# A decoder layer on one core: side loads on GpSimd's queue, and the cache rows copied from memory to memory

## The chip, the cores and the metric

The kernel runs on one core of one Trainium2 chip. Its time is the device time of one execution in microseconds (us). The core has a matrix engine (PE), a vector engine (DVE), a scalar engine (ACT), GpSimd (POOL) and a sync engine (SP) that here only issues DMAs. Each engine takes its instructions in a fixed order and waits at each for the semaphores that it needs. All DMAs of the core are carried by the same 16 DMA engines. Those that SP issues appear in the profile as queue q1 (`hardware_dynamic`), those that GpSimd issues as queue q0 (`software_dynamic`).

## The reference

One layer of a hybrid decoder, for a prompt of 256 tokens and a group of 8 sample tokens which share the weights, all in float32. Cut to what matters here:

```python
h = _rmsnorm(x, norm_mix)
q, k, v, z, xbc, dt, qm, g = jnp.split(h @ w_in, ...)         # one input projection
a_out = _swa_attend(q, k_all, v_all, ...)                     # window 128, grouped queries
s_out, conv_new, h_new = _ssd(xbc, z, dt, state_conv, state_ssm, ...)
m_out = _mem_attend(qm, mem_k, mem_v)                         # 256 memory tokens
merged = g0 * (a_out @ w_up_swa) + g1 * (s_out @ w_up_ssd) + g2 * (m_out @ w_up_mem)
x = x + merged @ w_out
y = x + (silu(h2 @ w_gate) * (h2 @ w_up)) @ w_down            # h2 = rmsnorm(x)
# of the sample group:
k_all = concat([cache_swa_k, k], axis=1); s_swa_k = k_all[:, 1:]   # 127 old rows move up by one
v_all = concat([cache_swa_v, v], axis=1); s_swa_v = v_all[:, 1:]
s_ssm = decay * state_ssm + dt * x * B                              # 32 x 64 x 128 per token
```

Each of the eight sample tokens has its own sliding-window cache (128 rows of 256 numbers for keys and as many for values), memory cache (256 rows of 1024 for keys and for values) and recurrent state. The outputs `s_swa_k` and `s_swa_v` are the window caches moved up by one row, with the new row at the end.

## The kernel before

**The stream.** The work on the weights is a list of units. A unit is a `raw` tile of 128 x 1024 numbers (512 KB), issued on SP in line L230. ACT copies it to `hi` (L167) and DVE computes `lo` (L168), which split each number in two parts of reduced precision. Then PE runs 24 products of 128 x 128 by 264 columns (L146; for the memory keys and values 12 of 512 columns). `feed` issues loads four units ahead and splits up to three ahead; there are four `raw`, three `hi` and three `lo` buffers. The order of the stream is: memory keys and values (`pmem`), the input projection (`pin`) with the branches' projections (`pua`, `pum`, `pus`) among it, then `pout` (w_out), and the feed-forward groups (`pg`, `pu`, `pdn`).

**The side work.** Norms, attention and the recurrent scan run beside the stream. They are generators in two queues, `side` and `slow`; after each unit they advance by a little. Their loads are the side loads: `x` for the norm (L408, 4 DMAs of 512 KB), and those of the generator `ahead` (L556), which fetches two tiles ahead: 32 tiles of the memory caches into `lm` buffers, and 4 tiles of the window caches and 16 of the recurrent state into `ld` buffers. In the notes below the state tiles are called j0 to j15. All of these are issued on SP, among the loads of weights. GpSimd issues the stores and the small loads and re-loads: `out_dram<-ld` (L1229) stores an updated state tile, `bb` and `cbs` (L1216, L1217) and `dec` (L1155) are broadcast reads, `mg_d`, `mgi`, `sg_d` and `sig` carry the gates and the merged sum out to DRAM and back, `xg` and `xgs` (L1438, L1440) fetch x again for the w_out stage.

**The rows that move up.** In `swa` (the window attention), the sample's key cache comes in two `ld` tiles of four tokens each, with the 128 rows on partitions; the value cache does the same later. As soon as such a tile is there, `move_rows` (L520) stores its partitions 1 to 127 to rows 0 to 126 of the output, on GpSimd.

**What sets the order.** The program is written in the order of the generators, but the instructions of every engine are then placed by a scheduler that plays the program through on its own costs. An engine's list is therefore fixed when the program is built, and it is not the order of the text: a load or a store is put where that planning had it ready. The two buffers `ld` hold in turn window-cache tiles and state tiles; a state load waits for the store of the tile two before it, since it reuses that buffer. A DMA of GpSimd also waits for the eighth DMA before it on that queue, with which it shares a semaphore.

Of the kernel before, what the change touches and what calls it, by code (L numbers as in the profile page):

```python
# [20 lines left out]
NP = 256          # prompt tokens  # L21
NS = 8            # sample tokens
NT = NP + NS      # columns of every activation
# [4 lines left out]
# column offsets of w_in  # L28
# [7 lines left out]
class Side:  # L36
    """Work that runs beside the stream of weights: tasks in a fixed order, a little after each unit."""
# [25 lines left out]
    def drain(self, name):  # L63
        """Everything up to and with the task of that name."""
        while any(t[0] == name for t in self.tasks):
            g = self._head()
            assert g is not None, (name, self.tasks[0])
            sum(g)
            self.tasks.pop(0)
# [3 lines left out]
def tile_hybrid_decoder_step(  # L73
# [42 lines left out]
    class Feat:  # L116
        """16 tiles of features, hi and lo, each [P, NT]"""
# [34 lines left out]
    def rsqrt(v, n, parts=P, alloc=None):  # L152
        """v ** -0.5 of positive v: an estimate from the exponent, then three Newton steps."""
        alloc = alloc or tiny
        y = alloc("rs_y", n)[0:parts]
        a = alloc("rs_a", n)[0:parts]
        V.tensor_scalar(y.bitcast(I32), v.bitcast(I32), 1, None, op0=ALU.logical_shift_right)
        V.tensor_scalar(y.bitcast(I32), y.bitcast(I32), -1.0, MAGIC, op0=ALU.mult, op1=ALU.add)
        for _ in range(3):
            V.tensor_tensor(a, y, y, op=ALU.mult)  # L160
            V.scalar_tensor_tensor(a, a, -0.5, v, op0=ALU.mult, op1=ALU.mult)
            V.scalar_tensor_tensor(y, a, 1.5, y, op0=ALU.add, op1=ALU.mult)
        return y

    def split(hi, lo, src):
        """src = hi + lo exactly, each with the 12 bits of float32r."""
        act(hi, src, AF.Copy)  # L167
        V.tensor_tensor(lo, src, hi.bitcast(F32), op=ALU.subtract)  # L168

    # ------------------------------------------------------------ constants  # L170
# [6 lines left out]
    # ------------------------------------------------------------ loads of the start  # L177
# [40 lines left out]
    # ------------------------------------------------------------ the stream of weights  # L218
# [40 lines left out]
    def group(name, loads, nk, xh, xl, after, perm=False, before=None):  # L259
        """Four output tiles: the sum over nk tiles of features of w^T x."""  # L260
        st = {}

        def prod(u):
            def f(hi, lo):
                if u == 0:
                    if before:
                        before()
                    st["ps"] = [dps(name)[:, 0:NT] for _ in range(4)]
                for c in range(4):
                    for k in range(2):  # L270
                        kk = 2 * u + k
                        wh = hi[:, k * 512 + c * P:k * 512 + (c + 1) * P]
                        wl = lo[:, k * 512 + c * P:k * 512 + (c + 1) * P]
                        mm(st["ps"][c], wh, xh(kk), start=kk == 0, stop=False)
                        mm(st["ps"][c], wh, xl(kk), start=False, stop=False)
                        mm(st["ps"][c], wl, xh(kk), start=False, stop=kk == nk - 1)
            return f

        for u in range(nk // 2):
            units.append(dict(  # L280
                loads=loads(u), perm=perm, prod=prod(u),
                after=(lambda: after(st["ps"])) if u == nk // 2 - 1 else None))
# [4 lines left out]
    # ------------------------------------------------------------ memory keys and values  # L287
# [112 lines left out]
    # ------------------------------------------------------------ h = RMSNorm(x), features on partitions  # L400
    hh, hl = Feat("hh"), Feat("hl")

    def prep_x():
        x_t = {}
        for h in range(2):
            for t in range(2):
                m = (lm if t else ld)("x")
                nc.sync.dma_start(m, x_prompt[0, t * P:(t + 1) * P, h * 1024:(h + 1) * 1024])  # L408
                x_t[t, h] = m
                yield 1.3  # L410
# [33 lines left out]
    # ------------------------------------------------------------ the other constants  # L444
    tri = const([P, P], "tri")              # tri[s, l] = l >= s
    nd = const([P, 256], "nd")              # -(distance) of a block's queries to the last 256 keys
# [16 lines left out]
    def consts():  # L463
# [36 lines left out]
        # the sample's convolution over its state  # L500
# [17 lines left out]
    def move_rows(dst, b, tile_):  # L518
        """Rows of a cache that move up by one, of four tokens of the sample."""
        nc.gpsimd.dma_start(dst[0, b:b + 4, 0:127].rearrange("b t h d -> t b (h d)"), tile_[1:128])  # L520


    # ------------------------------------------------------------ input projection
# [25 lines left out]
    # ---- the caches and the state, loaded ahead in the order in which they are used  # L549
    def ahead(sources, pool, depth):  # L550
        tiles = []
        for n in range(len(sources)):
            while len(tiles) < min(n + depth, len(sources)):
                b, src = sources[len(tiles)]
                t = pool("ld")
                nc.sync.dma_start(t.rearrange("p (b c) -> p b c", b=b) if b else t, src)  # L556
                tiles.append(t)
            yield tiles[n]
# [8 lines left out]
    # ---- memory attention  # L567
    def mem_prompt_work():
        qm = qt["qm"]
        # mean squares of the queries  # L570
# [16 lines left out]
        # the sample's, a row per token and head  # L587
# [20 lines left out]
        # the sample's queries as rows, and to all partitions  # L608
# [9 lines left out]
        # prompt  # L618
# [40 lines left out]
    def mem_sample_work():  # L659
        rq, qd = mT["rq"], mT["qd"]  # L660
        # scores by the vector engine, a key per partition
# [29 lines left out]
    def mem_sample_values():  # L691
        pT = mT["p"]
        po = sps("oms")
        for b in range(NS):
            # the heads' outputs of token b in row b of the heads' strips of 32 partitions
            w = t1("pb")[:, 0:256].rearrange("p (mc h e) -> p mc h e", mc=2, h=4)
            V.memset(w.rearrange("p mc h e -> p (mc h e)"), 0.0)
            V.tensor_copy(w[:, :, :, b], pT.rearrange("p (mc b h) -> p mc b h", mc=2, b=NS)[:, :, b])
            for mc in range(2):
                vc = next(mem_loads)  # L700
                for h in range(4):
                    mm(po[32 * h:32 * h + 32, 0:256], w[:, mc, h], vc[:, h * 256:(h + 1) * 256],
                       start=b == 0 and mc == 0, stop=b == NS - 1 and mc == 1)
                yield 1.5
# [11 lines left out]
    # ---- sliding-window attention  # L716
# [19 lines left out]
    def swa_keys():  # L736
        kvt = kvT["t"]
        # keys and values with tokens on partitions
# [47 lines left out]
    def swa():  # L786
# [3 lines left out]
        # mean squares of the queries  # L790
# [31 lines left out]
        # prompt  # L822
# [55 lines left out]
        # sample  # L878
        pT_s = sps("sTs")
        kcs = {}  # L880
        for b in range(NS):
            if b % 4 == 0:
                kc = next(other_loads).rearrange("p (b c) -> p b c", b=4)
                move_rows(s_swa_k, b, kc)
# [19 lines left out]
        # -(distance) of the sample to the cache  # L904
# [27 lines left out]
        for b in range(NS):  # L932
            if b % 4 == 0:
                vc = next(other_loads).rearrange("p (b c) -> p b c", b=4)
                move_rows(s_swa_v, b, vc)
            # a strip of 32 partitions for each token, its 16 heads first
            mm(po[32 * (b % 4):32 * (b % 4) + 32, b // 4], pT[:, 16 * b:16 * b + 32], vc[:, b % 4])
# [19 lines left out]
    # ------------------------------------------------------------ SSD  # L957
    ssd = {}
    dt_tok = const([P, 64], "dt_tok")
    last = const([P, 11, 24], "last")       # the raw rows that the next step's convolution needs  # L960
# [5 lines left out]
    def conv(ct, raw, dst):  # L966
        """dst = silu(conv(raw) + b) of the four tiles of channels from ct on; the last raw rows go out."""
# [61 lines left out]
    def softplus(x, n, rows):  # L1029
        """log(1 + exp(x)) = max(x, 0) + 2 atanh(u / (2 + u)), u = exp(-|x|)."""  # L1030
# [16 lines left out]
    def task_dt():  # L1047
# [16 lines left out]
        # sample: heads on partitions, then each head's values on the partitions of its channels  # L1064
# [19 lines left out]
        # cumulative sums of dt * a within the chunks  # L1084
# [9 lines left out]
        # weights of the states  # L1094
# [10 lines left out]
    def ssd_chunk_work(g):  # L1105
# [20 lines left out]
        # states  # L1126
# [55 lines left out]
    def ssd_norm_work(g):  # L1182
# [8 lines left out]
        # 64 tokens in each strip of 32 partitions  # L1191
# [106 lines left out]
    # ------------------------------------------------------------ gates and the branches' projections  # L1298
# [78 lines left out]
    # order of the stream  # L1377
# [55 lines left out]
    # ------------------------------------------------------------ x + merged @ w_out  # L1433
# [44 lines left out]

    for i in range(4):
        group("pout", w_loads(w_out[0], 512 * i), KT, lambda k: mg[k // 4][:, k % 4], lambda k: mg[k // 4][:, 4 + k % 4], after_out(i),  # L1480
              before=lambda i=i: load_x(i))

    # ------------------------------------------------------------ SwiGLU
# [61 lines left out]
    # ------------------------------------------------------------ run the stream  # L1545
# [65 lines left out]
```

## Time and profile before

| what | us |
|---|---|
| median of 3 runs | 2030.79 (2026.6 to 2030.96) |
| profiled execution, span from first to last instruction | 2028.6 |
| PE busy | 1947.4 (96%) |
| DVE busy | 1159.9 (57%) |
| ACT busy | 970.5 (48%) |
| POOL busy | 103.0 (5%) |
| moved by SP's DMAs (q1) | 353.5 MB |
| moved by GpSimd's DMAs (q0) | 45.0 MB |

The profile page gives the profiled execution's span and no other time of its own; the span lies 2.2 us under the median of the runs. A busy PE is an upper figure, since the ends of its pipelined products are modelled. What PE loses shows in three ways: as idle time, as a granted clock below 1, and as fewer instructions in a stretch of time. In the views by stretch a row has the stretch, its length, busy time (and number of instructions) of PE, PE's weight loads, DVE, ACT and POOL, the granted clock, the busy share of the DMA engines, and GB/s.

### The profile page before, as it was taken

The numbers are of one execution on the slowest core, as the hardware profiler recorded it, in microseconds if no ns is written. First come the engines' busy times: TensorE is split into PE (matmuls) and PEld (weight loads), VectorE is DVE, ScalarE is ACT, GpSimd is POOL, SyncE is SP. The second block draws the span as 40 slices with busy tenths as digits, with TensorE's granted clock in tenths as the row PEclk, the third lists the DMA queues.
The fourth block names the chain that finished last, engine by engine and source line by source line (L and its number), as shares of the span: only waits on it lengthen the run. The fifth ranks groups of instructions, "written<-read, shape, count | busy, mean of one in ns | idle before, by whom it ended". The sixth has DMA issues, their size and how long they took to land.

```text
span 2028.6 us, 37670 instructions
## 1 busy us (share of the span) xinstructions
PE 1947.4 (96%) x15436; PEld 1880.1 (93%) x15436; DVE 1159.9 (57%) x2217; ACT 970.5 (48%) x1419; POOL 103.0 (5%) x187
## 2 busy tenths in 40 slices
PE   8989999996999879899999999999999999999999
PEld 6778898885999779899999999999999999999998
DVE  5634667653667657568745556555544555445553
ACT  6634445753666556564544454444333444334443
POOL 2011000010001000111000000000000000000000
PEclk9999999997999889899999999999999999999999
DMA  8656666666758786978755555666556665556653
GB/s 276 197 184 172 227 210 222 189 183 214 207 158 240 208 225 199 244 238 292 246 177 191 194 175 169 179 185 177 183 181 178 181 179 180 185 179 179 184 186 130
DMA packets 214750, 400.90 MB, mean 198 GB/s; under 512 B 21143, under 2 KB 41798, under 8 KB 214440
## 3 DMA queue, kind: packets, MB, share of 16 engines
q1 hardware_dynamic: 193792, 353.50, 56.8%
q0 software_dynamic: 20784, 44.99, 8.2%
q8 instruction: 121, 1.98, 0.4%
q14 instruction: 53, 0.43, 0.1%
HBM read 374.45 MB, written 24.06 MB: 196 GB/s over the span
## 4 chain that ended last, share of the span: by engine, by line
PE 82%; DMA 10%; DVE 3%; issue 2%; ACT 2%; POOL 0%; SPq 0%; ACTq 0%; POOLq 0%; DVEq 0%
PE pin L146 22%; PE pu L146 13%; PE pdn L146 13%; PE pg L146 13%; PE pout L146 5%; PE pus L146 5%; PE pmem L146 5%; DMA ld<-in_state_ssm_dram 4%; PE pum L146 2%; DMA raw<-in_w_in_dram 2%; DVE lo L168 1%; DMA ld<-in_cache_mem_v_dram 1%; DVE ld L1225 1%; ACT hi L167 1%; PE po L146 1%
## 5 line engine op out<-in xcount | busy, mean ns | idle before, releaser
L168 DVE TENSOR_TENSOR lo<-raw,hi 128x1024 fp32r<-128x1024 f32 (+1 forms) x626 | 747.3, 1197 | 689.6 <-ACT hi L167 686.4
L167 ACT ACTIVATE hi<-raw 128x1024 fp32r<-128x1024 f32 (+1 forms) x626 | 645.4, 1036 | 883.2 <-PE pin L146 189.9
L146 PE MATMUL pin<-hh,hi 128*128 128x264 f32 x1728 | 499.9, 292 | 40.1 <-ACT hi L167 37.7
L146 PE MATMUL pin<-hl,hi 128*128 128x264 f32 x1728 | 497.6, 290 | 0.0
L146 PE MATMUL pin<-hh,lo 128*128 128x264 f32 x1728 | 487.7, 290 | 6.1 <-DVE lo L168 5.8
L146 PEld LDWEIGHTS pin<-hh,hi 128*128 128x128 f32 x1728 | 332.7, 193 | 47.4 <-ACT hi L167 39.9
L146 PEld LDWEIGHTS pin<-hh,lo 128*128 128x128 f32 x1728 | 325.7, 192 | 10.7 <-DVE lo L168 8.7
L146 PEld LDWEIGHTS pin<-hl,hi 128*128 128x128 f32 x1728 | 332.4, 192 | 3.3 <-issue 2.5
L146 PE MATMUL pdn<-fah,hi 128*128 128x264 f32 x704 | 200.0, 285 | 0.0
L146 PE MATMUL pdn<-fal,hi 128*128 128x264 f32 x704 | 199.7, 285 | 0.0
L146 PE MATMUL pu<-h2h,hi 128*128 128x264 f32 x704 | 199.7, 285 | 0.0
L146 PE MATMUL pu<-h2l,hi 128*128 128x264 f32 x704 | 199.5, 285 | 0.0
L146 PE MATMUL pg<-h2l,hi 128*128 128x264 f32 x704 | 199.3, 285 | 0.0
L146 PE MATMUL pg<-h2h,hi 128*128 128x264 f32 x704 | 198.7, 284 | 0.0
L146 PE MATMUL pdn<-fah,lo 128*128 128x264 f32 x704 | 197.3, 285 | 0.0
L146 PE MATMUL pu<-h2h,lo 128*128 128x264 f32 x704 | 196.9, 285 | 0.0
L146 PE MATMUL pg<-h2h,lo 128*128 128x264 f32 x704 | 196.4, 285 | 0.0
L146 PEld LDWEIGHTS pdn<-fah,hi 128*128 128x128 f32 x704 | 132.9, 189 | 0.1
L146 PEld LDWEIGHTS pu<-h2h,hi 128*128 128x128 f32 x704 | 132.9, 189 | 0.0
L146 PEld LDWEIGHTS pu<-h2l,hi 128*128 128x128 f32 x704 | 132.8, 189 | 0.0
L146 PEld LDWEIGHTS pdn<-fal,hi 128*128 128x128 f32 x704 | 132.7, 189 | 0.1
L146 PEld LDWEIGHTS pg<-h2h,hi 128*128 128x128 f32 x704 | 132.8, 189 | 0.0
(504 smaller groups left out, 2954.4 us busy)
## 6 DMA issues: line engine op xcount, KB each, us to landing
raw<-in_w_in_dram SPq DMA_DIRECT2D x218, 512.0 KB, 4.9
raw<-in_w_gate_dram SPq DMA_DIRECT2D x88, 512.0 KB, 3.7
raw<-in_w_up_dram SPq DMA_DIRECT2D x88, 512.0 KB, 4.1
raw<-in_w_down_dram SPq DMA_DIRECT2D x88, 512.0 KB, 3.8
raw<-in_w_mem_kv_dram SPq DMA_DIRECT2D x32, 512.0 KB, 5.1
raw<-in_w_up_ssd_dram SPq DMA_DIRECT2D x32, 512.0 KB, 3.8
raw<-in_w_out_dram SPq DMA_DIRECT2D x32, 512.0 KB, 3.7
ld<-in_cache_mem_k_dram SPq DMA_DIRECT2D x16, 512.0 KB, 5.0
```

Source lines behind the costliest of these rows:

```text
L146: nc.tensor.matmul(out, lhsT=lhsT, rhs=rhs, start=start, stop=stop)
L167: act(hi, src, AF.Copy)
L168: V.tensor_tensor(lo, src, hi.bitcast(F32), op=ALU.subtract)
L1225: V.scalar_tensor_tensor(h[:, b], bb[:, b], dx[:, b:b + 1], h[:, b], op0=ALU.mult, op1=ALU.add)
```

## The change

All side loads go out on GpSimd's queue, so that SP issues weights alone (and, as before, the first loads of the memory prompt and the last stores). `move_rows` no longer stores from the tiles; it copies both caches from DRAM to DRAM, once each, and is called from the w_out groups. The diff, without the comments that were dropped and with the lines around cut:

```diff
     def prep_x():
...
-                nc.sync.dma_start(m, x_prompt[0, t * P:(t + 1) * P, h * 1024:(h + 1) * 1024])
+                nc.gpsimd.dma_start(m, x_prompt[0, t * P:(t + 1) * P, h * 1024:(h + 1) * 1024])
...
-    def move_rows(dst, b, tile_):
-        nc.gpsimd.dma_start(dst[0, b:b + 4, 0:127].rearrange("b t h d -> t b (h d)"), tile_[1:128])
+    def move_rows():
+        for dst, src in ((s_swa_k, cache_swa_k), (s_swa_v, cache_swa_v)):
+            to, of = (t[0].rearrange("b t h d -> b (t h d)")[:, o:o + 127 * 256].rearrange("b (s e) -> s b e", s=16)
+                      for t, o in ((dst, 0), (src, 256)))
+            tc.keep_in_program_order(nc.gpsimd.dma_start(to, of))
...
     def ahead(sources, pool, depth):
...
-                nc.sync.dma_start(t.rearrange("p (b c) -> p b c", b=b) if b else t, src)
+                nc.gpsimd.dma_start(t.rearrange("p (b c) -> p b c", b=b) if b else t, src)
...
     def swa():
...
                 kc = next(other_loads).rearrange("p (b c) -> p b c", b=4)
-                move_rows(s_swa_k, b, kc)
...
                 vc = next(other_loads).rearrange("p (b c) -> p b c", b=4)
-                move_rows(s_swa_v, b, vc)
...
+    def before_out(i):
+        load_x(i)
+        if i == 3:
+            move_rows()
+
     for i in range(4):
         group("pout", ..., after_out(i),
-              before=lambda i=i: load_x(i))
+              before=lambda i=i: before_out(i))
```

Since the scheduler places every instruction anew, the lists of the engines tell where things now stand. SP has 632 rows where it had 688. In these lists a row has the line, the operation and out<-in with the numbers of the buffers, and what stands behind them is the shape.

The first place is GpSimd's list where the window attention's key tiles are stored. Before, the two stores of 127 partitions (L520) stood between the stores of the memory values `vm` and ahead of the sample's queries `qd`:

```order
L371 DMA out_dram<-km_687 128x512
L350 DMA out_dram<-vm_109 128x512 x2
L520 DMA out_dram<-ld_4425 127x4x256
L350 DMA out_dram<-vm_109 128x512 x2
L520 DMA out_dram<-ld_4427 127x4x256
L615 DMA qd<-qrow_1850 32x128 x2
```

And now:

```order
L371 DMA out_dram<-km_687 128x512
L559 DMA ld_4425<-in_cache_swa_k_dram 128x4x256
L559 DMA ld_2340<-in_cache_mem_k_dram 128x1024
L350 DMA out_dram<-vm_109 128x512 x4
L559 DMA ld_4427<-in_cache_swa_k_dram 128x4x256
L559 DMA ld_2342<-in_cache_mem_k_dram 128x1024
L618 DMA qd<-qrow_1850 32x128 x2
```

The stores of 127 partitions are gone, and the loads of the tiles stand in their place. The same holds for the value tiles further on.

The second place is the third group of up_mem, where GpSimd re-loads the merged sum (`mgi`), 23 rows before the end of its list. The two copies from DRAM to DRAM (L523) now stand here, ahead of the re-load for up_mem's third group:

```order
L1349 DMA mgi_9898<-mg_d 128x1056
L1441 DMA xgs_13187<-in_x_sample_dram 8x512
L1441 DMA xgs_13480<-in_x_sample_dram 8x512
L523 DMA out_dram<-in_cache_swa_k_dram 16x8x2032
L523 DMA out_dram<-in_cache_swa_v_dram 16x8x2032
L1349 DMA mgi_10150<-mg_d 128x1056
L1355 DMA mg_d<-sig_9897 128x1056
L1349 DMA mgi_10316<-mg_d 128x1056
```

Although the text calls them in the w_out stage, they wait for nothing that is computed, and the scheduler put them this early; before, `mgi` followed the two `xgs` directly.

The third place is the recurrent state of group 1 (tiles j6 to j9). On SP, the loads of the state stood among those of the weights; that piece before:

```order
L230 DMA raw_7750<-in_w_in_dram 128x2x512
L556 DMA ld_7519<-in_state_ssm_dram 128x8x128
L230 DMA raw_7780<-in_w_in_dram 128x2x512
L556 DMA ld_7703<-in_state_ssm_dram 128x8x128
L230 DMA raw_7841<-in_w_in_dram 128x2x512
L230 DMA raw_7879<-in_w_in_dram 128x2x512
L556 DMA ld_8387<-in_state_ssm_dram 128x8x128
L230 DMA raw_7910<-in_w_in_dram 128x2x512
```

Now they stand on GpSimd, among the stores of the tiles and the broadcast reads (j7 is `ld_7515`, j8 `ld_7699`, j9 `ld_8383`; the numbers moved by four):

```order
L1372 DMA mg_d<-sig_7365 128x1056
L559 DMA ld_7515<-in_state_ssm_dram 128x8x128
L1230 DMA out_dram<-ld_7282 128x8x128
L1230 DMA out_dram<-ld_7515 128x8x128
L1217 DMA bb_8379<-bc_d 128x8x128
L559 DMA ld_7699<-in_state_ssm_dram 128x8x128
L1218 DMA cbs_8380<-bc_d 128x8x128
L559 DMA ld_8383<-in_state_ssm_dram 128x8x128
L1156 DMA dec_8067<-acs_d 128x8x128
```

The load of j7 now stands ahead of the store of j6, that of j8 behind the store of j7. On ACT the first operation on j8 and on j9 moved back behind some splits of weights; before:

```order
L1224 ACTIVATE ld_7519<-ld_7519,dsc 128x128 x8
L167 ACTIVATE hi_7752<-raw_7720 128x1024
L998 ACTIVATE raw_7810<-pin_7542 128x264
L998 ACTIVATE raw_7810<-pin_7543 128x264
L1224 ACTIVATE ld_7703<-ld_7703,dsc 128x128 x3
L998 ACTIVATE raw_7810<-pin_7544 128x264
L1224 ACTIVATE ld_7703<-ld_7703,dsc 128x128 x5
```

and now, with j8 behind the copies of the projection's result (`raw_7806`, the raw input of the convolution):

```order
L1225 ACTIVATE ld_7515<-ld_7515,dsc 128x128 x8
L167 ACTIVATE hi_7670<-raw_7638 128x1024
L167 ACTIVATE hi_7718<-raw_7668 128x1024
L167 ACTIVATE hi_7748<-raw_7716 128x1024
L999 ACTIVATE raw_7806<-pin_7538 128x264
L972 ACTIVATE acc_7812<-raw_7806,vbc,cw 128x264
L999 ACTIVATE raw_7806<-pin_7539 128x264
L999 ACTIVATE raw_7806<-pin_7540 128x264
L167 ACTIVATE hi_7778<-raw_7746 128x1024
L999 ACTIVATE raw_7806<-pin_7541 128x264
L972 ACTIVATE acc_7812<-raw_7806,vbc,cw 128x264 x3
L167 ACTIVATE hi_7839<-raw_7776 128x1024
```

j7's operation moved forward by two splits, and those on j8 and j9 follow the last row here.

## The prediction

> **What bounds the kernel now.** I began with the page's span and the shares of the chain that ended last, then cut the span into stretches, and read the DMA view, the chain in order of time and the waits of each stretch that loses.
>
> ```profile
> span 2028.6 us, 37670 instructions
> PE 82%; DMA 10%; DVE 3%; issue 2%; ACT 2%; POOL 0%; SPq 0%; ACTq 0%; POOLq 0%; DVEq 0%
> ```
>
> PE's products are the bound; a tenth of the chain is transfers that PE could not wait out. The view by stretch (columns: stretch, length, busy time and instructions of five engines, granted clock, DMA share, GB/s) says where:
>
> ```profile
> core 0: us, PE busy (x) PEld busy (x) DVE busy (x) ACT busy (x) POOL busy (x), PEclk, DMA share, GB/s
> 112.00:193.00 81.00, 71.49 (x539) 66.69 (x538) 29.81 (x50) 28.03 (x41) 10.29 (x4) 0.94 0.58 170
> 429.00:476.00 47.00, 29.01 (x248) 25.37 (x247) 18.19 (x45) 15.96 (x23) 9.41 (x3) 0.82 0.60 148
> 640.00:682.00 42.00, 32.38 (x263) 31.02 (x262) 21.39 (x51) 20.86 (x44) 4.88 (x6) 0.91 0.80 197
> 720.00:752.00 32.00, 19.69 (x154) 18.88 (x153) 14.50 (x44) 15.69 (x38) 3.52 (x4) 0.90 0.83 207
> 827.00:855.00 28.00, 19.64 (x151) 19.22 (x150) 9.89 (x28) 12.17 (x27) 2.27 (x4) 0.88 0.89 214
> 930.00:1000.00 70.00, 69.20 (x596) 68.12 (x593) 58.42 (x171) 33.60 (x47) 10.00 (x16) 1.00 0.86 292
> 1000.00:1100.00 100.00, 100.00 (x822) 100.00 (x822) 50.22 (x67) 46.34 (x61) 0.73 (x1) 1.00 0.60 185
> ```
>
> From 1000 us on PE never stops: 8.22 products per us, so a unit of 24 takes 2.92 us. The change can win nothing there. The first two stretches hold the stores of the window caches' keys and values, the next three the recurrent state. The DMA views of the first two (the strip over the stretch in 40 slices, then the issues, with the median us to landing last):
>
> ```profile
> DMA  9994229999920004501827396799913554636363
> raw<-in_w_in_dram SPq DMA_DIRECT2D x20, 512.0 KB, 10.5
> out_dram<-ld POOLq DMA_DIRECT2D x2, 508.0 KB, 39.8
> ...
> GB/s 71 335 54 0 40 362 170 277 113 35 123 204 108 40 37 41 60 78 291 246 231 134 303 269 267 187 300 137 51 51 47 52 48 45 38 49 220 262 223 324
> ld<-in_cache_mem_v_dram SPq DMA_DIRECT2D x2, 512.0 KB, 21.7
> out_dram<-ld POOLq DMA_DIRECT2D x2, 508.0 KB, 37.0
> ```
>
> A store of 127 partitions takes 37.0 us for 508 KB (520,192 bytes), 14.1 GB/s, and beside it the strip falls to 0 to 2 tenths for whole runs of slices while PE has nothing to do. That is the pace of one DMA engine out of 16: whatever else needs that one waits behind the store, and the other 15 idle. The chain in time order (start, us, what) and two waits (us in all, times, longest) show who pays:
>
> ```profile
> 128.70 22.22 DMA raw<-in_w_in_dram
> ...
> 454.17 20.21 DMA ld<-in_cache_mem_v_dram
> ...
> 653.68 21.51 DMA ld<-in_state_ssm_dram
> ...
> 732.08 15.90 DMA ld<-in_state_ssm_dram
> ...
> 829.70 19.30 DMA ld<-in_state_ssm_dram
> PE oms L146 <- DMA ld<-in_cache_mem_v_dram: 16.2, 2, 14.7
> ACT ld L1224 <- DMA ld<-in_state_ssm_dram: 45.7, 11, 12.3
> ```
>
> Over the whole span the same transfers land sooner, which is the price they have undisturbed:
>
> ```profile
> raw<-in_w_in_dram SPq DMA_DIRECT2D x218, 512.0 KB, 4.9
> ld<-in_cache_mem_v_dram SPq DMA_DIRECT2D x16, 512.0 KB, 5.2
> ld<-in_state_ssm_dram SPq DMA_DIRECT2D x16, 512.0 KB, 8.5
> ```
>
> **The change part by part.** *The key stores go.* In 112 to 193 PE is idle for 81.0 - 71.5 = 9.5 us and loses (1 - 0.94) x 81 = 4.9 to the lowered clock: 14.4. Counted by instructions, 539 / 8.22 = 65.6, so 15.4 missing. The chain's weight load of 22.2 us, 4.9 elsewhere, is enough to empty four buffers (four units are 11.7). Bounds: 8 (the idle time less the first refill) to 15.4; I take 13, since nothing else in the stretch is slow.
>
> *The value stores go.* In 429 to 476 idle time is 18.0 and the clock's loss 0.18 x 47 = 8.5: 26.5; by count 47 - 30.2 = 16.8 (attention's products make the count uneven). The memory value tile comes in 20.2 us where 5.2 is usual, 15 less, which takes all of the 14.7 that PE waited for it. With the clock that is 23.2; 3 I leave, as that tile's buffer comes free only at 454.17. Bounds 14 to 26; I take 20.
>
> *The side loads leave SP's list.* The three state stretches have 9.6 + 12.3 + 8.4 = 30.3 us idle and 3.8 + 3.2 + 3.4 = 10.4 of clock. SP issues weights and state in one order, so a state load that waits for its `ld` buffer holds all weights behind it, and one in transit shares with them:
>
> ```profile
> L556 SPq DMA_DIRECT2D ld<-in_cache_mem_v_dram x16: 327/341/5687, 362.3 to 513.7; - x16
> raw<-in_w_in_dram SPq DMA_DIRECT2D x4, 512.0 KB, 18.4
> q0 software_dynamic: 761, 2.78, 48.8%
> ```
>
> (The last two are of 640 to 668: a weight took 18.4 us while q0 moved 2.78 MB, the broadcasts and stores of the scan.) Now the wait stands on POOL. What is behind it there is `cbs`, `dec`, the gates' re-loads and the next state store, not weights. But the state loads now share a queue with those broadcasts, and ACT's first operation on each tile still waits for its load. What remains late next is the state, with ACT in its wait and the splits behind it. Bounds: 40.7, all of it, to -5, a little worse than before. I take half of the idle time and none of the clock, 15.
>
> *What it adds.* 52 loads and two copies go to POOL, whose work is light, and four stores of some 4.6 us each leave it. Its neighbours in kind, GpSimd's loads of half a MB, land thus:
>
> ```profile
> PE 1947.4 (96%) x15436; PEld 1880.1 (93%) x15436; DVE 1159.9 (57%) x2217; ACT 970.5 (48%) x1419; POOL 103.0 (5%) x187
> xg<-in_x_prompt_dram POOLq DMA_DIRECT2D x4, 512.0 KB, 4.4
> qb<-qd POOLq DMA_DIRECT2D x8, 512.0 KB, 7.0
> L520 POOL DMA_DIRECT2D out_dram<-ld x4: 4577/4592/4598, 112.3 to 438.5; - x4
> ```
>
> Against 5.2 on SP, 4.4 to 7.0 is between 0.8 sooner and 1.8 later. Tiles are fetched two ahead, and most of that is covered; where two or three tiles miss the cover it costs 0 to 8, and I take 2. If the cover goes, each of the 20 tiles after the memory keys costs at most 1.8. SP's saved issues and POOL's new ones cost nothing: SP had only issues to do, POOL is busy 5% of the time. The four x loads move the same bytes at the start from another queue: I count nothing, up to 2 either way.
>
> *The two copies* stand ahead of the third re-load of `mgi`, and DVE's addition of it has its fixed place (the first row is of 930 to 1000):
>
> ```profile
> mgi<-mg_d POOLq DMA_DIRECT2D x7, 528.0 KB, 7.2
> ...
> 932.49 0.55 POOL L1348 DMA_DIRECT2D mgi<-mg_d  x1
> 948.40 1.26 DVE L1353 TENSOR_TENSOR sig<-sig,mgi 128x1056 f32<-128x1056 f32 x1
> ```
>
> They move 2 x 16 x 8 x 2032 x 4 = 2.08 MB each way. If they take T, `mgi` lands at about 932.5 + T + 7.2, is needed at 948.4, and two split units (5.8) cover PE: the cost is T - 14.5, not below 0. Nearest row: 2.78 MB on q0 in 28 us beside full traffic, so T = 21 and a cost of 6. Ends: 292 GB/s at a share of 0.86 means 340 when free, T = 6, cost 0; or only the free 14% of that, 48 GB/s, T = 44, cost 29. I take 6. DVE is the engine that waits, with `lo` behind it, so that a longer T is PE's loss one for one.
> A page of the Trainium skill bears on T: "DMA: Bandwidth & Descriptors", section "Why a DMA increments its semaphore by 16 and not by 1", says that the number of engines is the largest up to 16 that divides the slowest dimension of both sides: one for 127 partitions, sixteen for the 16 here. The 14.1 GB/s of the stores agrees; no run so far shows the copies. By that rule, sixteen times the stores' pace would be 225 GB/s, an estimate by which T is 9 us, the cost 0 and the gain 46 in place of 40.
>
> The sum: -13 - 20 - 15 + 2 + 6 = -40 on the span of 2028.6: 1988.6. The median of the runs, 2030.8, lies 2.2 above that span, so 1990.8; I say 1991.
>
> **The rivals.** *The state stays late.* State loads behind `bb`, `cbs` and `dec` on q0 are no sooner than on q1: the third term is 0 and the side loads cost 8. -13 - 20 + 0 + 8 + 6 = -19: 2012. For it: q0 carries half of the DMA time in 640 to 668. Against: the 18.4 us of the weights there, which no longer stand behind.
>
> *Slower: the copies run on few engines.* At 14.1 GB/s per engine, 2.08 MB takes 148 us on one and 74 on two. Without the copies the gain is 46, so they decide from T = 60 on, under 2.5 engines. Two engines give 74 - 14.5 - 46 = +13, 2044; one gives 148 - 14.5 - 46 = +87, 2118. For it: the stores did just that, and the one copy from DRAM to DRAM in the trace, 192 KB in 7.6 us, is 26 GB/s, by which T would be 80. Against: a load of half its size beside it takes 7.0, so that little of the 7.6 is pace, and the copies come in 16 rows, not 127:
>
> ```profile
> sc<-in_state_conv_dram POOLq DMA_DIRECT2D x3, 96.0 KB, 7.0
> out_dram<-in_state_conv_dram POOLq DMA_DIRECT2D x1, 192.0 KB, 7.6
> ```
>
>
> *GpSimd issues late under DVE.* If each state load waited for one DVE operation of 1.26 us ahead of it on the path, 16 of them take 20 back: 2011. Against: from 930 to 1000, with DVE busy for 58.4 of 70 us, GpSimd's `mgi` lands in 7.2 and SP's weights, as large, in 6.5:
>
> ```profile
> raw<-in_w_in_dram SPq DMA_DIRECT2D x21, 512.0 KB, 6.5
> ```
>
> The Trainium skill, "SBUF — State Buffer", section "SBUF: two separate sides", has this as a trap: GpSimd cannot write the descriptors of its DMAs while DVE runs certain copies in a faster mode that takes a shared port. It speaks against the change; the 0.7 us between the two queues bears out little of it.
>
> *Not what it says.* The stores were not what held the weights, or something else of q0 takes their part: within 4 us of 2031. Against it stand the empty strips, just as long as the stores.
>
> **How the numbers follow.** The forecast has 0.72, the state staying late 0.12, the copies on few engines 0.07, no change 0.05, issuing under DVE 0.04. 0.2%, some 4 us, is about what a measurement of this kernel tells from no change. Faster: 0.72 + 0.12 + 0.04 = 0.88. Slower: 0.07 + 0.01 of the fourth rival = 0.08; same 0.04. The forecast's own range is 1968 to 2010, by the bounds of its terms taken together (all five at their best would be near 1949, at their worst near 2051, neither likely). The range of 1970 to 2022 takes in the two rivals at 2011 and 2012 and copies at cost 29; outside stay the slower rival, no change, and 0.06 below it.
>
> **What would show it.** Right: no transfer of 37 us; no run of 0 to 2 tenths in the first two stretches; weights there landing in 4 to 6 us; PE's wait at `oms` under 4; ACT's wait for state, 45.7, down by a third or more; copies landing in 10 to 25 us, with a wait of up to 10 us at the DVE addition; the stage after 1000 us unchanged. Wrong: copies that need over 60 us with PE idle behind them (the slower rival); state loads from GpSimd that land in over 15 us with clocks still below 0.95 in the last three stretches (the first rival); idle PE in 429 to 476 without a store there (the fourth).

## The result, and the profile after

The changed kernel takes 1981.01 us (median of 4 runs, 1979.88 to 1982.88), the kernel before 2030.88 in the same comparison: a ratio of 0.9749, 95% interval 0.9734 to 0.9764. The forecast was 1991, so the gain was 10 us larger than forecast. The profiled execution's span went from 2028.6 to 1980.1, by 48.5 us.

First the page of the changed kernel: its span, the moved bytes by queue (packets, MB, share of 16 engines) and the chain's shares.

```profile
span 1980.1 us, 37652 instructions
...
q1 hardware_dynamic: 169856, 324.13, 53.4%
q0 software_dynamic: 20944, 74.23, 12.6%
...
PE 84%; DMA 7%; DVE 3%; issue 3%; ACT 1%; POOL 0%; SPq 0%; ACTq 0%; POOLq 0%
```

The share of transfers in the chain fell from 10 to 7%. In the page's list of DMA issues (KB each, median us to landing), the side loads and the two copies read:

```profile
ld<-in_cache_mem_v_dram POOLq DMA_DIRECT2D x16, 512.0 KB, 4.8
ld<-in_state_ssm_dram POOLq DMA_DIRECT2D x16, 512.0 KB, 7.1
...
out_dram<-in_cache_swa_k_dram POOLq DMA_DIRECT2D x1, 1016.0 KB, 7.9
out_dram<-in_cache_swa_v_dram POOLq DMA_DIRECT2D x1, 1016.0 KB, 10.6
```

A memory value tile took 5.2 us from SP and takes 4.8 from GpSimd, a state tile 8.5 and now 7.1. This is not yet a merit of GpSimd's queue: with the copies changed alone, all from SP (the first run below), they take 4.6 and 6.2, so it is the absence of the slow stores. The copies land 7.9 and 10.6 us after issue. The stretches of before, by the same clock times (columns as before):

```profile
112.00:193.00 81.00, 81.00 (x650) 77.49 (x649) 42.05 (x92) 34.78 (x55) 6.59 (x12) 1.00 0.67 202
429.00:476.00 47.00, 46.89 (x414) 42.28 (x413) 29.31 (x66) 24.21 (x38) 7.41 (x12) 1.00 0.84 270
640.00:682.00 42.00, 39.65 (x349) 39.08 (x349) 39.22 (x130) 25.14 (x42) 6.78 (x8) 1.00 0.80 250
682.00:720.00 38.00, 30.76 (x236) 29.78 (x236) 20.70 (x42) 24.82 (x47) 4.40 (x5) 0.91 0.84 215
1000.00:1100.00 100.00, 100.00 (x814) 99.44 (x813) 57.11 (x82) 42.88 (x56) 1.43 (x2) 1.00 0.60 188
```

In the first two PE hardly stops (0.1 us idle in all; 650 products where there were 539, 414 where there were 248) and the granted clock is 1.00. The state's part still loses, now at other clock times. Their DMA views (112 to 193, then 429 to 476):

```profile
DMA  2899891856756665675594677558170538899769
raw<-in_w_in_dram SPq DMA_DIRECT2D x24, 512.0 KB, 3.6
```

```profile
DMA  7999973999999999884979648889988389797187
raw<-in_w_in_dram SPq DMA_DIRECT2D x14, 512.0 KB, 4.6
```

Weights land in 3.6 and 4.6 us where they took 10.5 and 10.9, and no run of slices at 0 to 2 tenths is left.

Clock times drift apart between two traces, so a better account goes by work: both have the same 14,208 products of the stream, in the same order but for some neighbours that change places, and one compares the start of the k-th in each. The table is worked out so from the two traces; a difference that appears between two rows was won or lost there.

| products of the stream | ends before at (us) | changed kernel ahead by then (us) | won in it (us) |
|---|---|---|---|
| 0 to 400, memory keys and values | 116.0 | -1.2 | -1.2 |
| to 800, key stores | 184.0 | 14.9 | +16.1 |
| to 1100, sample's memory queries | 240.9 | 18.6 | +3.7 |
| to 2300 | 433.9 | 18.6 | 0 |
| to 2500, value stores | 493.2 | 39.9 | +21.3 |
| to 4900, recurrent state | 864.5 | 50.4 | +10.5 |
| to 5500 | 945.7 | 50.4 | 0 |
| to 5900, third group of up_mem on | 996.7 | 48.5 | -1.9 |
| the rest | | 48.5 | 0 |

### The profile page after: what moved, and what is told of

It is laid out like the page before. It is cut to its first block, busy times and chain, and to the rows that moved or that the text cites. A ratio compares the mean times of both kernels' runs of the same rounds, so it can differ in the third digit from the quotient of the medians.

```text
span 1980.1 us, 37652 instructions
## 1 busy us (share of the span) xinstructions
PE 1937.3 (98%) x15436; PEld 1871.3 (95%) x15436; DVE 1159.3 (59%) x2217; ACT 970.8 (49%) x1419; POOL 122.6 (6%) x241
## 3 DMA queue, kind: packets, MB, share of 16 engines
q0 software_dynamic: 20944, 74.23, 12.6%
## 4 chain that ended last, share of the span: by engine, by line
PE 84%; DMA 7%; DVE 3%; issue 3%; ACT 1%; POOL 0%; SPq 0%; ACTq 0%; POOLq 0%
PE pin L146 22%; PE pu L146 13%; PE pdn L146 13%; PE pg L146 13%; PE pout L146 5%; PE pus L146 5%; PE pmem L146 5%; DMA raw<-in_w_in_dram 3%; PE pum L146 2%; DMA ld<-in_state_ssm_dram 1%; DVE lo L168 1%; PE pua L146 1%; DVE ld L1226 1%; DMA acs_d<-acsT 1%; PE po L146 1%
## 5 line engine op out<-in xcount | busy, mean ns | idle before, releaser
L146 PE MATMUL pin<-hh,hi 128*128 128x264 f32 x1728 | 494.7, 289 | 15.8 <-ACT hi L167 15.6
L146 PEld LDWEIGHTS pin<-hh,hi 128*128 128x128 f32 x1728 | 328.4, 190 | 22.9 <-ACT hi L167 18.2
L146 PEld LDWEIGHTS pin<-hl,hi 128*128 128x128 f32 x1728 | 328.3, 190 | 3.3 <-issue 2.5
```

What stands on the lines that cost most here:

```text
L146: nc.tensor.matmul(out, lhsT=lhsT, rhs=rhs, start=start, stop=stop)
```

## The experiments

Theory A: the stores of 127 partitions hurt because each runs at the pace of one DMA engine, and the loads on GpSimd are worth only what the state shows. Theory B: the weights were late because SP's list carried the side loads. Each kernel was timed against the kernel before on the same chip.

**One part alone.** Copies only: the side loads stay on SP.

```diff
-                nc.gpsimd.dma_start(t.rearrange("p (b c) -> p b c", b=b) if b else t, src)
+                nc.sync.dma_start(t.rearrange("p (b c) -> p b c", b=b) if b else t, src)
```

(and the x loads likewise).

> The copies from DRAM to DRAM alone; all side loads stay on SP. If the stores of 127 partitions on one DMA engine were what stopped PE (theory A), the first two stretches win as in the changed kernel, 37 to 41 us together, and the state's 10 do not come: 1990 to 1996 us. If the weights were late because SP's list carried the side loads (theory B), most of the gain is missing: above 2010 us.

1991.83 us, ratio 0.9813 (0.9796 to 0.9829): theory A's case. By products the key and value parts win 19 and 22 us where the changed kernel wins 20 and 21, and the recurrent state wins about 1.5, not 10.5.

Loads only: the changed kernel with the old `move_rows` and its four calls.

```diff
...
-            tc.keep_in_program_order(nc.gpsimd.dma_start(to, of))
...
+        nc.gpsimd.dma_start(dst[0, b:b + 4, 0:127].rearrange("b t h d -> t b (h d)"), tile_[1:128])
```

> The side loads alone go to GpSimd; the stores of 127 partitions stay as before. Theory A: only the state's part comes, 8 to 12 us: 2019 to 2024 us, and the stretches of the key and value stores lose as before, or more, since the cache loads now queue behind these stores. Theory B: most of the gain, under 2005 us.

2039.87 us, ratio 1.0052 (1.0036 to 1.0068): slower than before, and slower than either theory had it. Theory B falls, and what A had only as an aside was the main thing. GpSimd's list there, around the value stores (start, us, instruction, and in brackets its idle time before and what ended it):

```profile
423.78 4.59 POOL L520 DMA_DIRECT2D out_dram<-ld  x1 [5.60 <-issue]
428.37 0.77 POOL L556 DMA_DIRECT2D ld<-in_cache_swa_v_dram  x1
429.14 0.25 POOL L906 IOTA ti<- 128x128 int32 x1
461.17 4.58 POOL L520 DMA_DIRECT2D out_dram<-ld  x1 [31.77 <-DMA ld<-in_cache_swa_v_dram]
465.74 1.10 POOL L556 DMA_DIRECT2D ld<-in_cache_mem_v_dram  x2
```

The DMA view of the same kernel from 429 to 500 (median us to landing):

```profile
ld<-in_cache_mem_v_dram POOLq DMA_DIRECT2D x4, 512.0 KB, 16.6
ld<-in_cache_swa_v_dram POOLq DMA_DIRECT2D x1, 512.0 KB, 32.1
```

The second value tile, issued right behind the first store, takes 32.1 us; its own store waits for it on GpSimd, and the memory values stand behind that. The value part loses 27 us against before, and the state's part wins 10.6 as in the changed kernel. The two halves of the change are no sum: loads on GpSimd cost 10 us while the slow stores are there, and bring 11 (1991.8 to 1981.0) once they are gone.

**Is it the one engine?** The kernel before, with each store in two.

```diff
-        nc.gpsimd.dma_start(dst[0, b:b + 4, 0:127].rearrange("b t h d -> t b (h d)"), tile_[1:128])
+        for lo_, hi_ in ((0, 112), (112, 127)):
+            nc.gpsimd.dma_start(dst[0, b:b + 4, lo_:hi_].rearrange("b t h d -> t b (h d)"), tile_[1 + lo_:1 + hi_])
```

> The kernel before, with each store of 127 partitions issued as two, of 112 and of 15 partitions; the same bytes from the same tiles, side loads on SP. Theory A (the pace of one DMA engine did the harm): they land in under 12 us instead of 37 and the time is that of copies alone, 1990 to 1997 us. Rival C (it is the stores themselves, their bytes at that moment or their 4.6 us of issue on GpSimd): no gain over 5 us, 2026 to 2036 us.

1991.23 us, ratio 0.9811 (0.9796 to 0.9826). The summary of that line:

```profile
L521 POOL DMA_DIRECT2D out_dram<-ld x8: 569/664/748, 111.9 to 419.2; - x8
DMA to landing us min/median/max: 4.9/5.6/6.9
```

The same bytes from the same tiles at the same place land in 5.6 us instead of 38, issue in 0.7 instead of 4.6, and the time is that of the copies. The number of partitions in the store was the whole of the first two terms. That one engine sets the pace agrees with the trace's landing marks, of which each DMA leaves 16, as many as there are DMA engines. Of the first key store of before, 15 come 13.0 to 15.4 us after issue and the last one after 40.0; of the first store of 112, all 16 come between 4.7 and 6.9. With the side loads on GpSimd (the loads-only kernel with this edit) the same stores do as well as the copies:

> Side loads on GpSimd as in the changed kernel, and the rows stored from the tiles, in two parts of 112 and 15 partitions, instead of copied from DRAM to DRAM. If only the pace of one engine mattered, and not where the rows come from or when: 1979 to 1984 us. If loads on GpSimd suffer from any store among them, as they did from those of 127 partitions: above 1990 us.

1980.55 us, ratio 0.9754 (0.9738 to 0.977).

**What the copies cost.** The changed kernel without the call of `move_rows()`, which leaves the rows that move up unwritten:

```diff
-        if i == 3:
-            move_rows()
```

> The changed kernel without the two copies, so that the rows that move up are not written. What it wins is the copies' price. By the prediction's term, 6 us: 1975 us. By the comparison of the two traces, which shows 2 us lost in the third group of up_mem: 1979 us. If the copies are hidden: 1981 us.

1980.0 us, ratio 0.9755 (0.974 to 0.9771), not told apart from the changed kernel's 0.9749. By products the changed kernel is 1.8 us ahead of this one up to `mgi` and 0.9 behind it from the end of that row on, 2.7 lost there. The price is 0 to 3 us, not 6.

The same copies in 127 rows:

```diff
-            to, of = (t[0].rearrange("b t h d -> b (t h d)")[:, o:o + 127 * 256].rearrange("b (s e) -> s b e", s=16) ...
+            tc.keep_in_program_order(nc.gpsimd.dma_start(dst[0, :, 0:127].rearrange("b t h d -> t b (h d)"), ...
```

> The changed kernel with the two copies cut into 127 rows of 8 x 1 KB instead of 16 of 8 x 8 KB; same bytes, same place in GpSimd's list. If the slowest dimension of 127 puts each on one DMA engine, as the stores were, each takes some 74 us, and the re-load of the merged sum behind them is late: by the prediction's slower rival 1981 + 133 = 2114 us if the queue keeps its order, near 2020 us if the copies only slow what shares their engine (four such stores cost 41 before). If the shape does not matter: 1981 us.

2080.34 us, ratio 1.0235 (1.0209 to 1.0261): 99 us for the shape of two access patterns. The slower rival, then, was real and one factor away, but by another road than it was told. GpSimd's list:

```profile
894.44 6.75 POOL L521 DMA_DIRECT2D out_dram<-in_cache_swa_k_dram  x1 [4.71 <-issue]
946.93 6.71 POOL L521 DMA_DIRECT2D out_dram<-in_cache_swa_v_dram  x1 [45.74 <-issue]
996.91 0.60 POOL L1348 DMA_DIRECT2D mgi<-mg_d  x1 [43.27 <-issue]
```

What DVE waited for from 870 to 1060 (us in all, times, longest), and two stretches by engine:

```profile
DVE sig L1353 <- DMA mgi<-mg_d: 94.1, 2, 93.0
```

```profile
900.00:960.00 60.00, 10.13 (x80) 9.59 (x79) 8.52 (x35) 3.78 (x4) 7.90 (x2) 0.64 0.20 38
960.00:1000.00 40.00, 0.00 (x0) 0.00 (x0) 0.00 (x0) 0.00 (x0) 3.09 (x5) 0.50 0.14 31
```

The re-load is not slow in transit (4.5 us in the chain): GpSimd did not issue it for 43 us, nor the second copy for 46, each time about until the copy ahead had landed (49.7 and 52.1 us). From 960 to 1000 us PE, DVE and ACT stand still. The same `issue` stood in the trace of before, ahead of its second key store:

```profile
153.01 4.60 POOL L520 DMA_DIRECT2D out_dram<-ld  x1 [34.98 <-issue]
```

Only the last 17 us of it are of this kind: the tile that it stores had itself landed only at 136.1. And it is no rule: the second value store of before went out at 438.5 while the first was in transit until 466, and in the loads-only kernel a load went out right behind such a store. What makes GpSimd stop stays open.

**Which side loads?** State on SP, the rest on GpSimd; and the reverse.

```diff
+                (nc.sync if b == NS else nc.gpsimd).dma_start(t.rearrange("p (b c) -> p b c", b=b) if b else t, src)
```

> The changed kernel with the 16 state loads back on SP; x and the caches stay on GpSimd. If the last 11 us of the gain come from the weights no longer standing behind state loads that wait for their buffer: 1990 to 1993 us, with a wait of the weights in the three state stretches. If they come from the cache loads: 1981 us.

1994.03 us, ratio 0.9817 (0.9801 to 0.9833).

```diff
+                (nc.gpsimd if b == NS else nc.sync).dma_start(t.rearrange("p (b c) -> p b c", b=b) if b else t, src)
```

(and x on SP).

> The changed kernel with x and the caches back on SP, the 16 state loads alone on GpSimd, the copies as changed. If the state loads are all of the last 11 us: 1979 to 1982 us, and the start loses 1 to 2 us less than with x on GpSimd. If the caches carry it: 1990 us.

1981.08 us, ratio 0.9754 (0.9738 to 0.9769). The 16 state loads are all of the last 11 us; x and the caches could have stayed where they were. By products the recurrent state's part wins 4.6 to 16.9 us in the nine changed kernels of this document that load it from GpSimd, and -3.3 to 1.5 in the four others. Is it enough that these loads leave SP's list?

```diff
+                (nc.scalar if b == NS else nc.gpsimd).dma_start(t.rearrange("p (b c) -> p b c", b=b) if b else t, src)
```

> The changed kernel with the 16 state loads issued from ACT's queue, neither SP nor GpSimd. If the last 11 us need only that the state is off SP's list: 1979 to 1985 us. If what helps is GpSimd, which can wait for a free buffer at no price, while a wait on ACT holds the splits: 1988 us or more.

1999.56 us, ratio 0.9841 (0.9822 to 0.986): it is not; the time is no better than with the state on SP. Nor is it that ACT stood there waiting for a free buffer: its longest wait of that kind ahead of these issues was 0.3 us. ACT's waits for the state and for weights from 540 to 900, in the kernel before:

```profile
ACT ld L1224 <- DMA ld<-in_state_ssm_dram: 41.8, 9, 12.3
...
ACT hi L167 <- DMA raw<-in_w_in_dram: 5.7, 2, 3.6
```

With the state on SP, and then on ACT:

```profile
ACT ld L1225 <- DMA ld<-in_state_ssm_dram: 41.9, 8, 15.1
...
ACT hi L167 <- DMA raw<-in_w_in_dram: 12.3, 4, 6.0
```

```profile
ACT ld L1225 <- DMA ld<-in_state_ssm_dram: 40.2, 10, 11.8
...
ACT hi L167 <- DMA raw<-in_w_in_dram: 17.0, 6, 4.2
```

And on GpSimd (the changed kernel):

```profile
ACT hi L167 <- DMA raw<-in_w_in_dram: 29.6, 11, 8.5
...
ACT ld L1225 <- DMA ld<-in_state_ssm_dram: 9.9, 6, 2.8
```

ACT waits just as long for the state when it issues the loads itself. From GpSimd most of that wait is gone, but the wait for weights has grown: the two rows together are 47.5 us before, 54.2 with the state on SP, 57.2 on ACT and 39.5 on GpSimd.

Two things differ there, and no run separates them. The first is when single loads land. The third load of group 1 (j8) went out at almost the same place, at 682.94 from GpSimd and at 686.71 from ACT, but landed after 13.4 and 20.8 us. The rows of that load alone, of the changed kernel and of the one with the state on ACT, and the queues of the latter's page (packets, MB, share):

```profile
L559 POOL DMA_DIRECT2D ld<-in_state_ssm_dram x1: 887/887/887, 682.9 to 682.9; - x1
DMA to landing us min/median/max: 13.4/13.4/13.4
```

```profile
L559 ACTq DMA_DIRECT2D ld<-in_state_ssm_dram x1: 374/374/374, 686.7 to 686.7; - x1
DMA to landing us min/median/max: 20.8/20.8/20.8
```

```profile
q0 software_dynamic: 18640, 65.84, 11.1%
q10 hardware_dynamic: 16640, 8.39, 1.5%
```

The 16 state loads are 16,640 packets on ACT's queue, 1040 each of some 500 bytes, which is a tile's run. On GpSimd's they are 20,944 - 18,640 = 2304, 144 each of some 3.6 KB. That fewer packets get through sooner beside the broadcast reads is argued and not shown: no run changed the packets alone. It does not hold for every load either. The fourth of group 0 (j5) takes 19.6 us from GpSimd, 21.3 from SP and 17.1 from ACT, and the median of the 16 is 7.1, 6.8 and 6.4.

The second is the order of ACT's list, which the scheduler makes anew for each kernel. Ahead of the first operation on j5 stand 189 splits in the changed kernel and 188 with the state on SP or on ACT; for j9 it is 209, 207 and 208. Where a split more stands ahead, ACT has it done when the load is late, and waits for a weight instead. At j5 ACT's wait for the state is 0 in the changed kernel and 6.6 us in the two others, though the load takes no less time than from ACT.

**What is still late.** The first stop of PE left in the state's part, at 516 us, hangs on ACT's wait for `dec`, which waits for a store of 32 KB (`acs_d`) behind the broadcast reads `bb` and `cbs`.

```diff
-        nc.gpsimd.dma_start(acs_d, ac)
+        nc.sync.dma_start(acs_d, ac)
```

> The changed kernel with one small store moved to SP: the cumulative sums (acs_d, 32 KB), which in the changed kernel land 12.25 us after issue behind two broadcast reads on GpSimd's queue, while ACT waits for them with the splits of weights behind it. If the queue's order is what makes it late, it lands in under 5 us, PE's stop at 516 us (6.4 and some 3.4 of lowered clock) goes, and the time is 1971 to 1976 us. If the wait is only handed to the next load (dec) or to another engine: 1979 to 1983 us.

1981.01 us, ratio 0.9751 (0.973 to 0.9772): no change. GpSimd's wait for that store, in this kernel:

```profile
514.04 1.77 POOL L1156 DMA_DIRECT2D dec<-acs_d  x2 [10.91 <-DMA acs_d<-acsT]
```

Issued from SP at 502.5, it still lands past 513. The place in GpSimd's queue is not what holds it. With `bb` and `cbs` on SP as well (the same edit in their two lines):

> As with the small store on SP, and the broadcast reads bb and cbs on SP as well, so that the state loads share GpSimd's queue with dec and the stores only. If state loads of 13 to 17 us (the third and fourth of each group) are late because of the order of that queue: they land in under 9 us and the time is 1965 to 1973 us. If it is the broadcast reads themselves, wherever they are issued: no better than with the small store alone, and worse by some us where they hold weights on SP.

1978.82 us, ratio 0.9741 (0.9718 to 0.9764), not told apart from the changed kernel. `bb` lands in 9.2 to 9.8 us there, and the five state loads that took 13 to 20 us (j5, j8, j9, j12, j13) take 8 to 12, which agrees with that queue's order being part of why they were late; but not all are under the 9 us expected, and PE's stop at 518 grew from 6.3 to 8.6. The two lowest together:

> Split stores in place of the copies, and bb, cbs and the small store on SP: the two variants that stood lowest beside the changed kernel (1980.6 and 1978.8), put together. If their differences to it are real and add up: 1975 to 1978 us. If both were noise: 1979 to 1983 us. Against the kernel before a gain of 2.4 to 2.8% by either.

1978.07 us, ratio 0.973 (0.9713 to 0.9748): beside the changed kernel's 0.9734 to 0.9764 the gain over it, if any, is under what these runs tell.

## Why the prediction was right, and where its steps were off

- **The key stores: 13 forecast, 16.1 + 3.7 measured.** The mechanism was right (copies only and split stores both show it). The term was mis-sized: the stretch was cut at 193, and what the stores did went on behind it. The sample's queries `qd` went out at 193.17 before and at 175.31 after, 17.9 sooner where the products were ahead by 14.9, and PE's wait of 4.1 us for the memory scores at 202, which hang on those, lay outside the stretch; after, two waits of 1.2 and 1.0 stand there.
- **The value stores: 20 forecast, 21.3 measured.** PE's `oms` products, which waited 14.7 us for one load, wait 0.6 in all for their loads.
- **The state: 15 forecast, 10.5 measured, and the step behind it failed.** The step was "a state load that waits for its `ld` buffer holds all weights behind it". Before, from 540 to 900, SP waited 10.8 us in all for `ld` buffers, at most 4.1 at once; ACT waited 5.7 us for those weights and 41.8 for the state, so weights held up on SP were not what cost the time; and issuing the state from ACT, which frees SP's list of it, brings nothing. Shown is that the gain comes with these 16 loads on GpSimd's queue. Whether by the landing of single loads or by the place of ACT's splits stays open. The sign that was named, ACT's wait for the state down by "a third or more", came true (41.8 to 9.9) and says less than it seems, since 23.9 us of it came back as a wait for weights.
- **The side loads' cost: 2 forecast, about 1.2 lost at the start**, where x comes from GpSimd. With x on SP the products are 2.6 us further at the end of that row. Some 60 products later 1.7 of these are made up, which is why the key stores' row is 16.1 with x on GpSimd and 14.4 with x on SP; the median shows nothing of it.
- **The copies: 6 forecast, 0 to 3 measured.** T was taken as 21 us from a stretch of broadcasts and stores; the copies landed in 7.9 and 10.6. The estimate that the rule of the Trainium skill gave ("DMA: Bandwidth & Descriptors", section "Why a DMA increments its semaphore by 16 and not by 1": the engines are the largest number up to 16 that divides the slowest dimension) was T = 9 and a cost of 0, and it was the better one. The 127 rows, on GpSimd's queue, agree with its other half: 1016 KB in 49.7 to 52.1 us, some 20 GB/s. The section also names an exception for some direct copies from GpSimd, by which 127 partitions would be spread over all 16 engines; the runs here do not show it.
- **The rivals.** Few engines would have made it slower: at 127 rows they did, 2080 where the rival gave 2118. The state staying late came true in part: two of the 16 loads still take over 15 us (19.6 and 17.4), and from 682 to 720 the clock is down to 0.91; but the third term was 10.5 and not 0. GpSimd starved under DVE (the Trainium skill, "SBUF — State Buffer", section "SBUF: two separate sides") was not seen: with DVE busy 59% of the span, memory keys, memory values and state land in 5.5, 4.8 and 7.1 us from GpSimd, and in 5.1, 4.6 and 6.2 from SP in the kernel with the copies alone, up to 0.9 later.

The sum: +19.8 + 21.3 + 10.5 - 1.2 - 1.9 = 48.5, against 40. That the forecast lies within 10 us is partly luck: the key stores were set 6.8 and the copies 4.1 too low in the gain, and the state 4.5 too high, by a step that failed.

## What to carry to other kernels

Look at the first number in the shape of every DMA: 127 cost 38 us in the stores, where 112 and 15 did as well as the copies, and 99 in the copies, where 16 cost 0 to 3; the sign in a profile is a strip of 0 to 2 tenths as long as one landing time. A slow transfer on GpSimd's queue can hold the loads behind it and GpSimd's later issues, so here loads were worth moving there only once nothing on it was slow; judged alone, that half of the change would have been thrown out. When a wait shrinks, look whether another one has grown by as much. Cut stretches by the work done, not by the clock, and let a stretch end only where PE has caught up.

## What the runs showed of the hardware

Behind a copy of 127 rows GpSimd stopped for 43 and 46 us at its next issue, with nothing that it waited for in the profile but `issue`; behind stores of 127 partitions it did so in one place and not in others. Of the 16 landing marks of such a store 14 or 15 came within 17 us and the last after 37 to 40. The same load of 512-byte runs is 1040 packets from SP or ACT and 144 from GpSimd. Broadcast reads of 512 KB from a few KB in DRAM take 9 to 19 us on either queue, and a store of 32 KB issued beside them took 10 to 12.
